# A two-block fp32 kernel on one core: last expert group summed in PSUM, GpSimd taken out of the combination, and another order in the MLP's last GEMM

## The chip, the cores and the metric

One core of a Trainium2 chip runs the whole program in one launch. The time is device microseconds (us) of one execution, the median of several; lower is better. The engines are PE (TensorE, matrix products), DVE (VectorE), ACT (ScalarE), POOL (GpSimd) and SP (SyncE, which here only issues transfers). All transfers of SP stand in one queue, those of POOL in another; an engine works through its own instructions in the order in which they were written for it.

## The reference, cut to what matters

The data are 512 rows of 1024 fp32 values. A first block mixes tokens and ends in a mixture of 64 experts (each row goes to 8 of them) beside a shared expert; a second block is attention and retention, and then an MLP with a squared ReLU.

```python
acc, _ = lax.scan(expert_block, jnp.zeros((N + 1, D), h.dtype), ...)   # rows gathered, SwiGLU, weighted, added back
f_lat = acc[:N] + swiglu(h, w_sh_gu, w_sh_down)
x_lat = x_lat + gt2 * rms_norm(f_lat, g_post_ffn)                      # end of block 1
...
h = x_lat
h = h + mixer_block(rmsnorm(h, norm_mix_gain), w_in, ...)              # block 2
h = h + jnp.square(jax.nn.relu(rmsnorm(h, norm_mlp_gain) @ w_ff1)) @ w_ff2
out = rmsnorm(h, norm_final_gain)
```

## The kernel before

**Products.** Every large product is made of three matmuls: each factor is split into a high part (`whi` for weights, written by ACT at L133; L153 for activations) and a low part (`wlo`, DVE L134; L154), and `mm3` adds high*high, low*high and high*low (L147 to L149). Weights come in units of 1 MB into a few buffers named `raw` (SP, L119), and a buffer is free for the next load when its unit is split. A unit splits in two pieces, so two `whi` and two `wlo` of 128x1024. The four tiles of 128 rows are numbered t = 0 to 3.

**End of the experts.** The experts run in groups. The outputs of a group (`ey`, 1024 columns a row) must be added to the rows that they came from. Columns 0 to 383 (`CA`) are added on PE: `expert_parts` splits them into `eys` (ACT and POOL), and a one-hot matrix `eoh` brings them into the PSUM tiles `acc[t]`. Columns 384 to 1023 go by indirect transfers of POOL that add into two tables `cb` in memory (L1076). Behind the last group stands a conditional loop for rows that found no place (`tc.If(total > 0)`, L1356 to L1359 in the profile), and then PE adds the shared expert's output product into `acc[t]` and a second PSUM tile `rest[t]` (48 matmuls of 128x512).

**The combination** is the start of the second block: for each tile the sums are put together from `acc[t]`, `rest[t]` (here `more[t]`) and the two reads of `cb` (into `cf` and `cg`), then normalised, scaled and added to the residual row `cx` (`x1[t]`), normalised again (`xn`), transposed on PE (`tp`, L1398) and split into the tiles `x`. It is written under `manual_schedule`: what each of DVE, ACT and POOL does there has the order of the code. `take(t)` empties PSUM, `norm(t)` scales and adds the residual, `normed_tile` makes `xn`, `turn_tile` transposes, `product(t, half)` is the first product of the block, with `w_v`. `rstd` is an inverse square root in 8 small DVE instructions for one column (11 for more).

```python
(nc.gpsimd if t else nc.vector).tensor_add(fs[t][:, CA:], fs[t][:, CA:], f2[t])
units = self.each_unit(wctx, self.quarters("w_v_2"), self.first_raws, [None, None, None, nc.gpsimd])
```

POOL so makes three of the four sums of the two tables (L1481), 384 of the 1024 columns of each residual add (`add2`, L1404) and the low part of the fourth `w_v` unit.

**The MLP** runs in four quarters of the hidden width. In each, `down` multiplies the hidden activations by a 1 MB x 4 block of `w_ff2` with seven products of half size (named 11, 3, 1, 2, 4, 12, 22) in place of eight. Sums of weight blocks are made by transfers that add into a loaded buffer (`plus`, issued by POOL, L1667). Products 11 and 2 collect in PSUM over the four quarters (`held`), the others are added to the output rows `h` quarter by quarter (`add`, L1682). In the last quarter the output is also squared (`ready`, `osq`, L1693), multiplied by the final gain (`gfin`, L1694), and each tile is scaled by its `rstd` (L1699 on DVE, L1700 on ACT) and sent out (SP, L1703, 8 transfers of 256 KB).

Of the kernel before, what the change touches and what calls it, by code (L numbers as in the profile page):

```python
# [11 lines left out]
F = mybir.dt.float32  # L12
R = mybir.dt.float32r
# [3 lines left out]
AF = mybir.ActivationFunctionType  # L17
OP = mybir.AluOpType
# [48 lines left out]
class Kernel:  # L67
# [1011 lines left out]

    def expert_parts(self, mp, y, row):  # L1080

        nc = self.nc
        m = row.shape[0]
        yh, yl = (mp.tile([128, CA], R, tag=f"eys{i}", name="eys", bufs=2)[0:m] for i in range(2))
        nc.scalar.activation(yh, y[0:m, :CA], AF.Copy)  # L1085
        last = nc.gpsimd.tensor_sub(yl, y[0:m, :CA], yh.bitcast(F))  # L1086
# [10 lines left out]
    def shared_expert(self, mp, pp, gp, gT, h2T):  # L1097
# [4 lines left out]
        for h in range(2):  # L1102
            hs = slice(h * H, (h + 1) * H)
            sg = []
            for u in range(2):
                for j in range(2):
# [9 lines left out]
                    yield  # L1116
    def shared_out(self, ps, gT, w, t, half):

        c = slice(half * 512, (half + 1) * 512)
        for i in range(2):  # L1120
            self.mm3(ps, [z[:, i, t * 128:(t + 1) * 128] for z in gT], [z[:, i, c] for z in w],
                     half == 1 and i == 0, i == 1)

# [86 lines left out]
    def experts(self, mp, pp, h2d, cb, acc, shared, gT, sums, grow, ahead, extra):  # L1210
# [84 lines left out]
        for t in range(NT):  # L1295
            nc.tensor.matmul(acc[t], zr[:, 0:128], zr, start=True, stop=False)
        late, sums = None, []
        for g in range(len(groups) + 1):
# [17 lines left out]
            def finish():  # L1316

                if not outs:
                    return
                e, parts = outs.pop(0)  # L1320
                lg = late[0]
                self.expert_out(pp, dn(e), [p[1:] for p in parts])
                last = None
                if not outs:
                    add()
                    for b, i in enumerate(rows_of[lg]):
                        s, last = self.expert_parts(mp, y[b], tabs[i][0])
                        sums.append(s)
# [44 lines left out]
        for t in range(NT):  # L1373
            self.shared_out(acc[t], gT, w, t, 0)
            rest.append(pp.tile([128, 512], F, tag="mm", name="mm", bufs=4))
            self.shared_out(rest[t], gT, w, t, 1)
        return rest
# [15 lines left out]
    def turn_tile(self, pp, xn, hi, lo, t):  # L1393
        ts = slice(t * 128, (t + 1) * 128)
        for u in range(2):
# [3 lines left out]
            self.split_ps(hi[:, 4 * u:4 * u + 4, ts], lo[:, 4 * u:4 * u + 4, ts], ps)  # L1399

    def add2(self, dst, a, b):

        for sl, e in ((slice(0, ADD_COLS), self.nc.vector), (slice(ADD_COLS, D), self.nc.gpsimd)):
            e.tensor_add(dst[:, sl], a[:, sl], b[:, sl])  # L1404

# [35 lines left out]
    def second_block(self, x1d, cb, acc, more, release):  # L1441
# [10 lines left out]
        with right("comb") as wp, ExitStack() as wctx:  # L1452
            fs = [wp.tile([128, D], F, name=f"cf{t}") for t in range(NT)]
            f2 = [wp.tile([128, D - CA], F, name=f"cg{t}") for t in range(NT)]

# [5 lines left out]
            def sums(t):  # L1461
                nc.sync.dma_start(fs[t][:, CA:], cb[0][rows[t], :])
                nc.sync.dma_start(f2[t], cb[1][rows[t], :])
# [7 lines left out]
            for t in range(1, NT):  # L1471
                nc.sync.dma_start(x1[t], x1d[rows[t], :])
            units = self.each_unit(wctx, self.quarters("w_v_2"), self.first_raws, [None, None, None, nc.gpsimd])
            ET = mybir.EngineType
            with tc.manual_schedule(engines={ET.DVE, ET.Activation, ET.Pool}):
                w = [next(units), next(units)]

                def take(t):

                    nc.scalar.activation(fs[t][:, 0:CA], acc[t][:, 0:CA], AF.Copy)  # L1480
                    (nc.gpsimd if t else nc.vector).tensor_add(fs[t][:, CA:], fs[t][:, CA:], f2[t])  # L1481
                    nc.vector.tensor_add(fs[t][:, CA:512], fs[t][:, CA:512], acc[t][:, CA:])
# [6 lines left out]
                take(0)  # L1489
                squares(fs[0], ss[:, 0:1])  # L1490
                nc.vector.tensor_mul(y, fs[0], g3)
# [4 lines left out]
                take(1)  # L1496
                xn = wp.tile([128, D], F, tag="xn", name="xn", bufs=2)
                nc.vector.tensor_scalar(xn, y, self.rstd(wp, ss0, D), None, op0=OP.mult)
                for t in range(2, NT):
                    take(t)  # L1500
                for t in range(1, NT):
                    squares(fs[t], ss[:, t:t + 1])
                release()
                pp = ctx.enter_context(tc.tile_pool(name="b2ps", bufs=1, space=PSUM))
                rs = self.rstd(wp, ss[:, 1:], D)
                self.turn_tile(pp, xn, xs[0], xs[1], 0)
                nc.sync.dma_start(xd[rows[0], :], x1[0])

                def norm(t):
                    nc.vector.scalar_tensor_tensor(fs[t], fs[t], rs[:, t - 1:t], g3, op0=OP.mult, op1=OP.mult)  # L1510
                    self.add2(x1[t], x1[t], fs[t])
                    nc.sync.dma_start(xd[rows[t], :], x1[t])
# [4 lines left out]

                norm(1)
                w.append(next(units))
                xn = self.normed_tile(wp, x1[1], gain)  # L1520
                w.append(next(units))
                w = [w[:2], w[2:]]
# [129 lines left out]
    def down(self, pp, rp, left, q, acc, held, gf):  # L1652
# [24 lines left out]

        def add(r, c, op, xs):
# [5 lines left out]
        def ready(r, c, last):  # L1684

            if q < 3:
                return
            for t in (2 * r, 2 * r + 1):
                if t not in ss:
                    ss[t] = rp.tile([128, 2], F, name=f"fss{t}")  # L1690
                a = acc[:, t, c * 512:(c + 1) * 512]
                sq = rp.tile([128, T], F, tag="relu", name="osq", bufs=6)
                nc.scalar.activation(sq, a, AF.Square, accum_out=ss[t][:, c:c + 1])  # L1693
                nc.vector.tensor_mul(a, a, gf[:, c * 512:(c + 1) * 512])  # L1694
                if last:
                    s = ss[t]
                    nc.vector.tensor_add(s[:, 0:1], s[:, 0:1], s[:, 1:2])
                    rs = self.rstd(rp, s[:, 0:1], D)
                    nc.vector.tensor_scalar(acc[:, t, 0:512], acc[:, t, 0:512], rs, None, op0=OP.mult)  # L1699
                    nc.scalar.activation(acc[:, t, 512:], acc[:, t, 512:], AF.Copy, scale=rs)  # L1700
                    for half in range(2):
                        sl = slice(half * 512, (half + 1) * 512)
                        nc.sync.dma_start(self.out[t * 128:(t + 1) * 128, sl], acc[:, t, sl])  # L1703

        e, f = load(0, 0), load(0, 1)
        plus(f, 1, 1)
        w = split(e)
        plus(e, 0, 1)
        product("11", w, held[0])
        z = product("3", split(f))  # L1710
        add(1, 1, "-", z)
        add(1, 0, "+", z)
        w = split(e)
        plus(e, 1, 1)
        z = product("1", w)
        add(1, 1, "-", z)
        add(0, 1, "-", z)
        w = split(e)
        plus(e, 1, 0)
        product("2", w, held[1])  # L1720
        if q == 3:
            add(0, 0, "+", held[0])
            x = [rp.tile([128, T], F, tag="relu", name="x", bufs=6) for _ in range(2)]
            for z, a, b in zip(x, *held):
                nc.scalar.activation(z, a, AF.Copy)
                nc.vector.tensor_add(z, b, z)
            add(1, 1, "-", x)
            ready(1, 1, False)
            add(0, 1, "-", x)
            add(1, 0, "+", x)  # L1730
        add(0, 1, "-", product("4", split(load(1, 1))))
        ready(0, 1, False)
        add(0, 0, "+", product("12", split(load(1, 0))))
        ready(0, 0, True)
        add(1, 0, "+", product("22", split(e)))
        ready(1, 0, True)

# [206 lines left out]
RAW3 = 2  # L1944
ADD_COLS = 640

# [141 lines left out]
```

## Time and profile before

| | |
|---|---|
| median of 3 runs | 2087.61 us (2087.3, 2087.61, 2090.02) |
| profiled execution: its time / its span in the profile | 2089.45 / 2087.7 us |
| granted clock of PE, mean (1.00 is 2.4 GHz) | 0.982 |
| PE busy | 1969.7 us, 94% of the span |
| DVE / ACT / POOL busy | 73% / 55% / 25% |

PE sets the pace nearly everywhere. The 118 us in which it is idle lie at the start and in a few joints between stages; the two places that the change touches are such joints.

### The profile page before, as it was taken

How to read it: one execution, taken by the hardware profiler on the slowest of the kernel's cores; microseconds unless marked ns; L12 is line 12 of the kernel's file. 1: busy time of each engine (PE TensorE's matmuls, PEld its weight loads, DVE VectorE, ACT ScalarE, POOL GpSimd, SP SyncE). 2: the span in 40 equal slices, each digit the busy share in tenths (PEclk: the TensorE clock that was granted, in tenths of full speed). 3: DMA queues.
4: the chain of work that ended last, by engine and by line, in shares of the span. 5: the costliest groups of instructions: out<-in, count | busy, mean ns of one | idle time of the engine just before them, and what ended most of it. 6: DMA issues, size and time to landing. Idle time of an engine off the chain costs nothing. (4 is left out here: it accounts for less than half of the span.)

```text
span 2087.7 us, 27579 instructions
## 1 busy us (share of the span) xinstructions
PE 1969.7 (94%) x9935; PEld 1583.8 (76%) x9935; DVE 1524.8 (73%) x2689; ACT 1156.2 (55%) x1734; POOL 512.1 (25%) x291
## 2 busy tenths in 40 slices
PE   7999999999889999899999996999999999999997
PEld 4877888787877677667766775777788888888886
DVE  6667766657899899899999997456863345755657
ACT  6544433233368798788888885334232324554554
POOL 0322221101236465445634323111100000000000
PEclk9999999999899999999999998999999999999999
DMA  7201126543489999899998997411122234546553
GB/s 294 80 22 43 68 98 252 212 166 132 168 302 349 312 343 351 284 353 340 353 347 306 330 333 252 143 61 61 41 91 91 99 143 134 159 126 197 123 140 81
DMA packets 73167, 406.03 MB, mean 194 GB/s; under 512 B 11758, under 2 KB 12735, under 8 KB 31428
## 3 DMA queue, kind: packets, MB, share of 16 engines
q1 hardware_dynamic: 58084, 360.18, 46.7%
q0 software_dynamic: 14944, 44.06, 9.7%
q8 instruction: 79, 1.29, 0.2%
q14 instruction: 60, 0.49, 0.1%
HBM read 388.07 MB, written 24.86 MB: 198 GB/s over the span
## 5 line engine op out<-in xcount | busy, mean ns | idle before, releaser
L134 DVE TENSOR_TENSOR wlo<-raw,whi 128x1024 fp32r<-128x1024 f32 x610 | 745.7, 1249 | 176.2 <-ACT whi L133 171.5
L133 ACT ACTIVATE whi<-raw 128x1024 fp32r<-128x1024 f32 x616 | 631.0, 1055 | 291.6 <-PE mm L148 178.5
L1076 POOL DMA_INDIRECT cb<-ey,sgi x67 | 151.6, 2262 | 158.8 <-ACT ey L1072 139.7
L1086 POOL TENSOR_TENSOR eys<-ey,eys 128x384 fp32r<-128x384 f32 (+2 forms) x47 | 102.9, 2191 | 126.4 <-ACT eys L1085 126.2
L147 PE MATMUL mm<-hT,whi 128*128 128x512 f32 x320 | 127.1, 397 | 0.6 <-DVE yb L369 0.6
L148 PE MATMUL mm<-hT,whi 128*128 128x512 f32 x320 | 125.9, 394 | 0.0
L149 PE MATMUL mm<-hT,wlo 128*128 128x512 f32 x320 | 125.5, 392 | 0.0
L148 PE MATMUL mm<-x,whi 128*128 128x512 f32 x304 | 122.5, 403 | 0.0
L147 PE MATMUL mm<-x,whi 128*128 128x512 f32 x304 | 120.9, 398 | 0.0
L149 PE MATMUL mm<-x,wlo 128*128 128x512 f32 x304 | 120.9, 398 | 0.0
L1034 PE MATMUL mm<-wlo,xT 128*128 128x512 f32 (+1 forms) x280 | 114.4, 409 | 4.1 <-DVE wlo L134 3.9
L1034 PE MATMUL mm<-whi,xT 128*128 128x512 f32 (+1 forms) x280 | 113.1, 404 | 0.3 <-ACT ey L1072 0.3
L148 PE MATMUL mm<-wlo,eaT 128*128 128x512 f32 (+2 forms) x268 | 106.6, 399 | 1.1 <-DVE wlo L134 0.9
L147 PE MATMUL mm<-whi,xT 128*96 128x512 f32 (+1 forms) x256 | 105.5, 412 | 0.3 <-DVE esum L1047 0.3
L148 PE MATMUL mm<-wlo,xT 128*96 128x512 f32 (+1 forms) x256 | 102.7, 401 | 3.1 <-DVE wlo L134 3.1
L149 PE MATMUL mm<-whi,eaT 128*128 128x512 f32 (+2 forms) x268 | 105.1, 394 | 0.0
L147 PE MATMUL mm<-whi,eaT 128*128 128x512 f32 (+2 forms) x268 | 101.7, 396 | 3.3 <-ACT eaT L153 1.7
L982 POOL DMA_INDIRECT xg<-h2d,sgi x47 | 79.8, 1699 | 97.9 <-issue 28.9
L147 PE MATMUL mm<-y,whi 128*128 128x512 f32 (+2 forms) x272 | 103.2, 379 | 0.0
L149 PE MATMUL mm<-y,wlo 128*128 128x512 f32 (+2 forms) x272 | 103.1, 379 | 0.0
L148 PE MATMUL mm<-y,whi 128*128 128x512 f32 (+2 forms) x272 | 103.1, 379 | 0.0
L149 PE MATMUL mm<-whi,xT 128*96 128x512 f32 (+1 forms) x256 | 101.3, 396 | 0.0
(591 smaller groups left out, 4684.9 us busy)
## 6 DMA issues: line engine op xcount, KB each, us to landing
raw<-in_w_expert_gu SPq DMA_DIRECT2D x128, 1024.0 KB
raw<-in_w_expert_down SPq DMA_DIRECT2D x64, 1024.0 KB
raw<-in_w_in SPq DMA_DIRECT2D x41, 1024.0 KB
raw<-in_w_ff SPq DMA_DIRECT2D x32, 1024.0 KB
raw<-in_w_ada SPq DMA_DIRECT2D x24, 1024.0 KB
raw<-in_w_ff POOLq DMA_DIRECT2D x16, 1024.0 KB
raw<-in_w_out SPq DMA_DIRECT2D x8, 1024.0 KB
raw<-in_w_v SPq DMA_DIRECT2D x4, 1024.0 KB
```

Of the source, the lines that this page charges most:

```text
L133: nc.scalar.activation(hi, rv[:, k:k + n], AF.Copy)
L134: (engine or nc.vector).tensor_sub(lo, rv[:, k:k + n], hi.bitcast(F))
L147: mm(ps, ah, bh, start=start, stop=False)
L148: mm(ps, ah, bl, start=False, stop=False)
L149: mm(ps, al, bh, start=False, stop=stop)
L982: self.nc.gpsimd.indirect_dma_start(out=xg[0:gi.shape[0]], out_offset=None, in_=h2d, in_offset=bass.IndirectOffsetOnAxis(ap=gi, axis=0), b ...
L1034: nc.tensor.matmul(ps[0:xT[0].shape[2]], xT[0][:, kk], z[:, k], start=kk == i == 0, stop=kk == KD - 1 and i == 1)
L1076: self.nc.gpsimd.indirect_dma_start(out=cb, out_offset=bass.IndirectOffsetOnAxis(ap=gi, axis=0), in_=y[p0:p1, CA:], in_offset=None, bounds ...
L1086: last = nc.gpsimd.tensor_sub(yl, y[0:m, :CA], yh.bitcast(F))
```

## The change

Part 1: if the last expert group is a single set of rows (here it has 96), all its 1024 columns are summed on PE (`whole`): ACT and DVE split them into `eyw`, nothing of this group goes to `cb`, and 16 matmuls of 128x512 behind the conditional loop (`ends`) take the place of 8 of 128x384 ahead of it. Part 2: in the combination POOL has no work any more. ACT alone empties PSUM, DVE makes the sums of the tables and all 1024 columns of the residual, squares and `rstd` are made tile by tile inside `norm`, and the third and fourth `w_v` units are split on DVE. Part 3: `down` has another order: the sums of weight blocks are made in the second buffer (`f`) in place of the first, products run as 11, 3, 2, 1, 4, 12, 22, and in the last quarter DVE and ACT follow the written order; one `rstd` serves two tiles, and the output leaves in 4 transfers of 512 KB.

```diff
-    def shared_out(self, ps, gT, w, t, half):
+    def shared_out(self, ps, gT, w, t, half, start):
...
+                if whole(lg):
+                    return
...
+            for half, ps in enumerate((acc[t], rest[t])):
+                for n, (oh, ys) in enumerate(ends):
+                    for i, y in enumerate(ys):
+                        nc.tensor.matmul(ps, oh[:, t * 128:(t + 1) * 128], y[:, half * 512:(half + 1) * 512],
+                                         start=half == 1 and n == i == 0, stop=False)
+                self.shared_out(ps, gT, w, t, half, half == 1 and not ends)
...
-            units = self.each_unit(wctx, self.quarters("w_v_2"), self.first_raws, [None, None, None, nc.gpsimd])
+            units = self.each_unit(wctx, self.quarters("w_v_2"), self.first_raws)
...
-                    nc.scalar.activation(fs[t][:, 0:CA], acc[t][:, 0:CA], AF.Copy)
-                    (nc.gpsimd if t else nc.vector).tensor_add(fs[t][:, CA:], fs[t][:, CA:], f2[t])
-                    nc.vector.tensor_add(fs[t][:, CA:512], fs[t][:, CA:512], acc[t][:, CA:])
-                    nc.vector.tensor_add(fs[t][:, 512:], fs[t][:, 512:], more[t])
+                    nc.scalar.activation(fs[t][:, 0:512], acc[t], AF.Copy)
+                    nc.scalar.activation(fs[t][:, 512:], more[t], AF.Copy)
+
+                def add(t):
+
+                    nc.vector.tensor_add(f1[t], f1[t], f2[t])
+                    nc.vector.tensor_add(fs[t][:, CA:], fs[t][:, CA:], f1[t])
...
+                def norm(t, between=None):
+                    add(t)
+                    squares(fs[t], ss[:, t:t + 1])
+                    if between:
+                        between()
+                    rs = self.rstd(wp, ss[:, t:t + 1], D)
+                    nc.vector.scalar_tensor_tensor(fs[t], fs[t], rs, g3, op0=OP.mult, op1=OP.mult)
+                    nc.vector.tensor_add(x1[t], x1[t], fs[t])
...
+            e, f = load(0, 0), load(0, 1)
+            plus(f, 1, 1)
+            w1, w3 = split(e), split(f)
+            plus(e, 0, 1)
+            plus(f, 0, 0)
+            product("11", w1, held[0])
+            w2 = split(f)
+            plus(f, 1, 0)
+            z = product("3", w3)
+            w = split(e)
...
+            for i in range(2):
+                t = 2 * r + i
+                if i:
+                    nc.vector.tensor_scalar(acc[:, t], acc[:, t], rs[:, i:i + 1], None, op0=OP.mult)
+                else:
+                    nc.scalar.activation(acc[:, t], acc[:, t], AF.Copy, scale=rs[:, i:i + 1])
+                nc.sync.dma_start(self.out[t * 128:(t + 1) * 128, :], acc[:, t])
```

How the instructions stand on three queues, before and after:

SP, behind the expert loop, where the last `w_v` load, the reads of `cb` and the first load of the attention's weights (`in_w_in`) are issued; before:

```order
L119 DMA raw<-in_w_v 128x2048
L1462 DMA cf_13584<-cb_93 128x640
L1463 DMA cg_13588<-cb_94 128x640
L1466 DMA g_13592<-g3d 128x1024
L1467 DMA cx_13593<-x1d 128x1024
```

and now:

```order
L119 DMA raw<-in_w_v 128x2048
L119 DMA raw<-in_w_in 128x2048
L1471 DMA cg_13595<-cb_93 128x640
L1472 DMA cg_13599<-cb_94 128x640
L1475 DMA g_13603<-g3d 128x1024
L1476 DMA cx_13604<-x1d 128x1024
```

The load of `in_w_in`, which stood behind the store `xd<-cx` of tile 0, has moved ahead of all reads of `cb`.

DVE, from the normalised tile 1 (`xn`) to the split of its transposed form (`x`), before:

```order
L1390 SCALAR_TENSOR_TENSOR xn<-cx_13595,rsy,gmix 128x1024
L1510 SCALAR_TENSOR_TENSOR cf_13587<-cf_13587,rsy,g_13592 128x1024
L1404 TENSOR_TENSOR cx_13596<-cx_13596,cf_13587 128x640
L154 TENSOR_TENSOR x_13576<-tp,x_13575 128x4x128 x2
L178 TENSOR_SCALAR rsx<-nss 128x1
```

and now (the line of dots stands for the other seven instructions of an `rstd`):

```order
L1404 SCALAR_TENSOR_TENSOR xn<-cx_13605,rsy,gmix 128x1024
L1494 TENSOR_TENSOR cg_13597<-cg_13597,cg_13601 128x640
L1495 TENSOR_TENSOR cf_13593<-cf_13593,cg_13597 128x640
L178 TENSOR_SCALAR rsx<-css 128x1
...
L1524 SCALAR_TENSOR_TENSOR cf_13593<-cf_13593,rsy,g_13603 128x1024
L1525 TENSOR_TENSOR cx_13606<-cx_13606,cf_13593 128x1024
L154 TENSOR_TENSOR x_13583<-tp,x_13582 128x4x128 x2
```

Between `xn` and the split of tile 1 stand now the sums of tile 2 and an `rstd` that needs ACT's squares of that tile.

DVE, the last instructions of the last `down`, before (the line of dots stands for small instructions of two `rstd`):

```order
L1694 TENSOR_TENSOR h<-h,gfin 128x512
L179 TENSOR_SCALAR rsy<-rsx 128x1
L1697 TENSOR_TENSOR fss_19599<-fss_19599 128x1
L182 SCALAR_TENSOR_TENSOR rsz<-rsy,rsx 128x1
L186 SCALAR_TENSOR_TENSOR rsy<-rsz,rsy 128x1
L1682 TENSOR_TENSOR h<-h,mm 128x512
...
```

and now:

```order
L1720 TENSOR_SCALAR h<-h,rsy 128x1024
L1695 TENSOR_TENSOR h<-h,mm 128x512
L1710 TENSOR_TENSOR h<-h,gfin 128x512
L1695 TENSOR_TENSOR h<-h,mm 128x512
L1710 TENSOR_TENSOR h<-h,gfin 128x512
L1715 TENSOR_TENSOR fss_19675<-fss_19675 128x2
```

Where the sums of the last product stood among the small instructions of the `rstd` of single tiles, both now stand together ahead of one `rstd` for two tiles.

## Rows read from the trace of the kernel before

**Rows 1.** Waits of PE, 1270 to 1350 us: total, times, longest.
```profile
PE tp L1398 <- DMA xd<-cx: 12.8, 1, 12.8
PE tp L1398 <- DVE xn L1390: 2.8, 1, 2.8
```

**Rows 2.** Waits of PE, 1750 to 2087 us.
```profile
PE tp L1398 <- DVE xn L1390: 0.3, 1, 0.3
```

**Rows 3.** Busy time by stretch: PE, PEld, DVE, ACT, POOL, clock, DMA share, GB/s.
```profile
1270.00:1280.00 10.00, 9.01 (x39) 6.93 (x37) 3.23 (x6) 1.64 (x3) 0.00 (x0) 1.00 0.94 328
1280.00:1290.00 10.00, 0.00 (x0) 0.00 (x0) 9.41 (x21) 3.44 (x7) 5.41 (x3) 0.62 1.04 413
...
1350.00:1750.00 400.00, 395.24 (x1860) 317.71 (x1859) 218.69 (x427) 127.96 (x214) 36.08 (x26) 1.00 0.25 86
```

**Rows 4.** SP's issues, timeline: start, duration, instruction.
```profile
1256.71 10.99 SPq L119 DMA_DIRECT2D raw<-in_w_v  x4
1271.10 0.33 SPq L1462 DMA_DIRECT2D cf<-cb  x1
```

**Rows 5.** DVE's timeline, end of the experts to the transposed tile 1.
```profile
1268.92 1.22 DVE L134 TENSOR_TENSOR wlo<-raw,whi 128x1024 fp32r<-128x1024 f32 x1 [0.44 <-DVEq L1356]
1276.76 0.82 DVE L1481 TENSOR_TENSOR cf<-cf,cg 128x640 f32<-128x640 f32 x1 [6.62 <-DMA cg<-cb]
...
1279.85 0.15 DVE L178 TENSOR_SCALAR rsx<-css 128x1 f32<-128x1 f32 x1
...
1281.57 1.28 DVE L714 SCALAR_TENSOR_TENSOR cx<-rv,rsy,cx 128x1024 f32<-128x1024 f32 x1
1282.89 2.50 DVE L1495 TENSOR_TENSOR rv<-cx,gmix 128x1024 f32<-128x1024 f32 x1
...
1289.23 0.75 DVE L1498 TENSOR_SCALAR xn<-rv,rsy 128x1024 f32<-128x1024 f32 x1
...
1293.30 0.17 DVE L178 TENSOR_SCALAR rsx<-css 128x3 f32<-128x3 f32 x1 [1.73 <-ACT rv L1486]
...
1295.36 1.28 DVE L154 TENSOR_TENSOR x<-tp,x 128x512 fp32r<-128x512 f32 x2
...
1310.79 1.28 DVE L154 TENSOR_TENSOR x<-tp,x 128x512 fp32r<-128x512 f32 x2
```

**Rows 6.** POOL's timeline in the same stretch.
```profile
1282.77 5.50 POOL L1481 TENSOR_TENSOR cf<-cf,cg 128x640 f32<-128x640 f32 x3 [15.63 <-DMA cf<-cb]
```

**Rows 7.** ACT's timeline: one square of a tile.
```profile
1290.89 1.06 ACT L1486 ACTIVATE rv<-cf 128x1024 f32<-128x1024 f32 x1 [3.44 <-DVE cf L1483]
```

**Rows 8.** PE's timeline: three idle times and the matmuls behind them.
```profile
1278.62 0.39 PE L149 MATMUL mm<-whi,shT 128*128 128x512 f32 x1
1291.78 1.94 PE L1398 MATMUL tp<-ident,xn 128*128 128x128 f32 x8 [12.77 <-DMA xd<-cx]
...
1308.96 1.27 PE L1398 MATMUL tp<-ident,xn 128*128 128x128 f32 x8 [2.83 <-DVE xn L1390]
...
854.76 1.01 PE L1095 MATMUL acc<-eys,eoh 96*128 96x384 f32 x2 [6.39 <-POOL eys L1086]
855.57 0.63 PE L1034 MATMUL mm<-wlo,xT 128*128 128x512 f32 x1
...
859.41 0.40 PE L148 MATMUL mm<-wlo,xT 128*128 128x512 f32 x1
```

**Rows 9.** PE's timeline, the last matmul.
```profile
2074.06 0.39 PE L149 MATMUL mm<-whi,hdx2l 128*128 128x512 f32 x1
```

**Rows 10.** ACT's timeline in the last quarter.
```profile
2048.17 5.80 ACT L133 ACTIVATE whi<-raw 128x1024 fp32r<-128x1024 f32 x6 [5.00 <-DMA raw<-in_w_ff]
...
2077.57 0.63 ACT L1693 ACTIVATE osq<-h 128x512 f32<-128x512 f32 x1 [1.42 <-DVE h L1682]
...
2083.16 0.72 ACT L1700 ACTIVATE h<-h,rsy 128x512 f32<-128x512 f32 x1 [1.56 <-DVE rsy L186]
```

**Rows 11.** POOL's timeline, an adding transfer of the last quarter.
```profile
2040.26 0.86 POOL L1667 DMA_DIRECT2D raw<-in_w_ff  x1 [22.36 <-DVE hd1l L154]
```

More of the change, by code (lines that the diff above doesn't have):

```diff
@@ L1078, in expert_send, with expert_parts @@
                                           compute_op=OP.add)
-    def expert_parts(self, mp, y, row):
+    def expert_parts(self, mp, y, row, whole=False):
         nc = self.nc
         m = row.shape[0]
-        yh, yl = (mp.tile([128, CA], R, tag=f"eys{i}", name="eys", bufs=2)[0:m] for i in range(2))
-        nc.scalar.activation(yh, y[0:m, :CA], AF.Copy)
-        last = nc.gpsimd.tensor_sub(yl, y[0:m, :CA], yh.bitcast(F))
+        if whole:
+            yh, yl = (mp.tile([128, D], R, tag="ey", name="eyw", bufs=3)[0:m] for _ in range(2))
+            for c in range(0, D, 512):
+                sl = slice(c, c + 512)
+                nc.scalar.activation(yh[:, sl], y[0:m, sl], AF.Copy)
+                last = nc.vector.tensor_sub(yl[:, sl], y[0:m, sl], yh[:, sl].bitcast(F))
+        else:
+            yh, yl = (mp.tile([128, CA], R, tag=f"eys{i}", name="eys", bufs=2)[0:m] for i in range(2))
+            nc.scalar.activation(yh, y[0:m, :CA], AF.Copy)
+            last = nc.gpsimd.tensor_sub(yl, y[0:m, :CA], yh.bitcast(F))
         oh = mp.tile([128, T], R, tag="eoh", name="eoh", bufs=2)[0:m]
@@ L1116, in shared_expert @@
                     yield
-    def shared_out(self, ps, gT, w, t, half):
+    def shared_out(self, ps, gT, w, t, half, start):
         c = slice(half * 512, (half + 1) * 512)
         for i in range(2):
-            self.mm3(ps, [z[:, i, t * 128:(t + 1) * 128] for z in gT], [z[:, i, c] for z in w],
-                     half == 1 and i == 0, i == 1)
+            self.mm3(ps, [z[:, i, t * 128:(t + 1) * 128] for z in gT], [z[:, i, c] for z in w], start and i == 0, i == 1)
     def first_block(self):
@@ L1296, in experts @@
             nc.tensor.matmul(acc[t], zr[:, 0:128], zr, start=True, stop=False)
-        late, sums = None, []
+        late, sums, ends = None, [], []
+        whole = lambda g: g == len(groups) - 1 and len(groups[g][1]) == 1
         for g in range(len(groups) + 1):
@@ L1326, in finish @@
                     for b, i in enumerate(rows_of[lg]):
-                        s, last = self.expert_parts(mp, y[b], tabs[i][0])
-                        sums.append(s)
+                        s, last = self.expert_parts(mp, y[b], tabs[i][0], whole(lg))
+                        (ends if whole(lg) else sums).append(s)
+                if whole(lg):
+                    return
                 with tc.issue_after(last.ins) if last else ExitStack():
@@ L1453, in second_block @@
             fs = [wp.tile([128, D], F, name=f"cf{t}") for t in range(NT)]
-            f2 = [wp.tile([128, D - CA], F, name=f"cg{t}") for t in range(NT)]
+            f1, f2 = ([wp.tile([128, D - CA], F, name=f"cg{i}{t}") for t in range(NT)] for i in range(2))
             sq, y = vr[:, 3], vr[:, 2]
@@ L1489, in second_block @@
                 take(0)
+                add(0)
                 squares(fs[0], ss[:, 0:1])
+                for t in range(1, NT):
+                    take(t)
+                release()
+                pp = ctx.enter_context(tc.tile_pool(name="b2ps", bufs=1, space=PSUM))
                 nc.vector.tensor_mul(y, fs[0], g3)
@@ L1676, in product, with add @@
             return pss
-        def add(r, c, op, xs):
+        def add(r, c, op, xs, then=None):
             for i, x in enumerate(xs):
@@ L1682, in add @@
                 (nc.vector.tensor_add if op == "+" else nc.vector.tensor_sub)(a, a, x)
[L1684 to L1736, printed above, removed]
+                if then:
+                    then(2 * r + i)
+        def ready(c):
+            return lambda t: squares(t, c)
+        def squares(t, c):
+            r, i = divmod(t, 2)
+            if r not in ss:
+                ss[r] = rp.tile([128, 2, 2], F, name=f"fss{r}")
+            a = acc[:, t, c * 512:(c + 1) * 512]
+            sq = rp.tile([128, T], F, tag="relu", name="osq", bufs=6)
+            nc.scalar.activation(sq, a, AF.Square, accum_out=ss[r][:, c, i:i + 1])
+            nc.vector.tensor_mul(a, a, gf[:, c * 512:(c + 1) * 512])
@@ new lines, in down @@
+        ET = mybir.EngineType
+        end = q == 3
+        with self.tc.manual_schedule(engines={ET.DVE, ET.Activation}) if end else ExitStack():
+            e, f = load(0, 0), load(0, 1)
[8 more added lines that the diff above has]
+            w = split(e)
+            add(1, 1, "-", z)
+            add(1, 0, "+", z)
+            product("2", w2, held[1])
+            w4 = split(load(1, 1))
+            if end:
+                add(0, 0, "+", held[0])
+                x = [rp.tile([128, T], F, tag="relu", name="x", bufs=6) for _ in range(2)]
+                for z, a in zip(x, held[0]):
+                    nc.scalar.activation(z, a, AF.Copy)
+            z1 = product("1", w)
+            z4 = product("4", w4)
+            wg = split(load(1, 0))
+            if end:
+                for z, b in zip(x, held[1]):
+                    nc.vector.tensor_add(z, b, z)
+                add(0, 1, "-", x)
+                add(1, 1, "-", x)
+            add(0, 1, "-", z1)
+            add(1, 1, "-", z1, end and ready(1))
+            if end:
+                add(1, 0, "+", x)
+            wl = split(f)
+            add(0, 1, "-", z4, end and ready(1))
+            add(0, 0, "+", product("12", wg), end and ready(0))
+            if end:
+                result(0)
+            add(1, 0, "+", product("22", wl), end and ready(0))
+            if end:
+                result(1)
@@ L1944 @@
 RAW3 = 2
-ADD_COLS = 640
 CA = 384
```

26 lines of the change are left out of this document (7 added, 19 removed).

## The prediction

> **What bounds the kernel now.** I read the page first (PE busy 94% of the span), then PE's waits by stretch, since only a place where PE waits, or the end behind its last matmul, can give or cost time. Between 1270 and 1350 us PE waits twice, 12.8 us for the first transposition of the combination and 2.8 us for the second [rows 1]; from 1750 us to the end it waits 0.3 us in all [rows 2]. So there are two places to cost. The combination is a chain of DVE and ACT from the landing of the `cb` tables to `xn` (the wait view names the store of `cx` as releaser of the first transposition, but the last reader of the PSUM that the transposition needs is `take(3)` on DVE, which ends just ahead of it). The tail lies behind the last matmul, which ends at 2074.06 + 0.39 = 2074.45 [rows 9] in a span of 2087.7: 13.25 us of DVE, ACT and the output. In the MLP between them PE is never late, so no order of `down` can gain there; it can only lose.
>
> **The change, part 1: where the tables land.** Before, SP issues the first read of `cb` at 1271.10 [rows 4] and DVE has both tables at 1276.76, 5.66 us later [rows 5]. Now a load of 1 MB stands ahead of the reads, and it needs the buffer of a `w_v` unit to be split. DVE's last split piece behind the conditional loop ends at 1268.92 + 1.22 = 1270.14 [rows 5]; the two `eyw` pieces push one more `wlo` behind the loop, so the unit is split 1.2 us later, 1271.3, and the reads are issued at about 1271.7, 0.6 us later than before. What the 1 MB ahead costs no row shows. Below, nothing: the transfers of this queue already overlap, and the last group's own adding transfer is gone; the tables land at 1276.76. Above, the whole MB passes first at the 328 GB/s of this stretch [rows 3], 3.2 us, so 1276.76 + 0.6 + 3.2 = 1280.5. I take the middle, X = 1278.6, since the queue was also full before (a `w_v` load was 4 us old when the reads were issued).
>
> The Trainium skill, "DMA: Bandwidth & Descriptors", section "Queues, rings and completion order", says that on each transfer engine the descriptors of one issuing queue are consumed in ring order. Taken strictly, that gives the upper bound. The trace of before has no large load directly ahead of a waited-for read, so it can't decide here; it is the third rival below.
>
> **Part 2: from X to the first transposition.** DVE and ACT must do: two sums of 640 columns (0.82 each, 1.64), a square (1.06 [rows 7] and its read-out, 1.25), `rstd` (from 1279.85 to 1281.57 [rows 5], 1.72), the residual (1.28), the next square (1.25), `rstd` (1.72) and `xn` (0.75 [rows 5]): 9.6, with half a microsecond of hand-overs 10.1. The multiply by the gain lies beside the square: it took 2.50 us while POOL made its three sums of 5.50 us [rows 5, 6], where a `wlo` of the same 1024 columns takes 1.22, so POOL's work had cost it 1.3 us; that is gone. PSUM is emptied by ACT early: the shared products, now 64 matmuls in place of 48, end 16 x 0.23 = 3.7 us after the last one of before (1278.62 [rows 8]), less about 0.7 because 8 matmuls ahead of the loop are gone: 1282, and `take(3)` ends by 1283. So the first transposition comes at 1278.6 + 10.1 = 1288.7, in place of 1291.78: 3.1 us gained. An earlier X gives little more: behind `take(3)` ACT's square, `rstd` and `xn` still take 3.7, so it can't start before 1286.7.
>
> **Part 3: from the first to the second transposition, and what gives it back.** DVE now has more to do between them: the split of tile 0 (3.0 with the transposition), sums of tile 1 (1.6), ACT's square and the first `whi` (2.3, since the third `w_v` unit waits for ACT behind that square), two `wlo` (2.4), `rstd` (1.7), scale and residual (2.5), two `wlo` of the unit that POOL had (2.4), `rstd` (1.7), `xn` (1.3): 18.9 us, against 1308.96 - 1291.78 = 17.2 before [rows 8]. The second transposition so comes at 1307.6, 1.4 us earlier than before. But then the split of the transposed tile 1, which stood 3.3 us behind the start of `xn` (1310.79 [rows 5]), has to let pass on DVE: the sums of tile 2 (1.6), ACT's square (1.25), `rstd` (1.7), scale and residual (2.5), 7 us. It ends its first half at 1315.2. Before, the nine last products of tile 0 stood behind the second transposition and kept PE at work (at half clock) until about 1313.3, when tile 1 was there; now all 48 stand ahead of it, PE has nothing else, and tile 1's products start at 1315.3, 2.0 us later. PE has then been idle, but for eight transpositions, since 1306, and restarts at the low clock: after an idle time of 6.39 us at 854.76 the matmuls took 0.63 in place of 0.40 (1.2 in place of 2.4 GHz) until 859.41 [rows 8], 4.65 us of half speed, 2.3 us lost. About 1.0 comes back, since two products that need only the high part of tile 1 run early and one matmul fewer stands before the third transposition. Sum of the combination: 2.0 + 2.3 - 1.0 = **+3.3 us**; with the bounds of X (-1.8, +1.9) +1.5 to +5.2. In the attention behind it PE is busy 395.24 of 400 us [rows 3], so the shift stays.
>
> **Part 4: the tail.** The last product ends as before, 2074.45. DVE is free of the older work then (two `rstd` chains and four scalings less), so both last sums stand at 2073.85 and 2075.1 (the second waits for its PSUM and the first `gfin`), the last `gfin` ends at 2076.3, ACT's square (0.63 [rows 10] and 0.18) at 2076.55. One `rstd` of eleven small instructions takes 2.1 (from 1293.30 to 1295.36 [rows 5]) and a sum of 0.2 stands ahead: 2078.9. Then ACT scales 1024 columns, estimated at 1.15 from 0.72 for 512 [rows 10], DVE 0.75: ready at 2080.1. Before, ACT was ready at 2083.16 + 0.72 = 2083.88 [rows 10], and the span ended 3.8 us later. Now the last two tiles (1 MB) leave together where 0.5 MB did: 0.5 MB more at 413 GB/s [rows 3] is 1.3, at 328 GB/s 1.6. End: 2080.1 + 3.8 + 1.4 = 2085.3, **-2.4 us**; bounds -1.0 (DVE a microsecond late, slower output) to -3.0.
>
> **Part 5: the four `down` before that end** I cost at nothing. An adding transfer lands 7.9 us after its issue (2040.26 to ACT's release at 2048.17 [rows 10, 11]). The sum for product 2 is issued behind the split of unit 3, near 2027.6, and lands near 2035.5; its split is done by 2038, product 2 starts near 2047. The cover is thus 9 us in the last quarter. The loads and adding transfers per quarter are as many as before.
>
> Sum: 3.3 - 2.4 = +0.9 on a span of 2087.7. The profiled execution took 2089.45, 1.84 over the median; the shift is taken on the median: 2087.61 + 0.9 = **2088.5 us**. Its own range, by the bounds above: 2086.1 to 2091.8.
>
> **Rivals.**
> 1. *Faster, 0.15: tile 1 does not wait so long.* If X is at its lower bound (+1.5) and the idle time ahead of tile 1's products, broken by the transpositions, does not cost the clock (-2.3), and the tail gives 3.0, the sum is -3.8: 2083.8. For it: half of that idle time lies on either side of the transpositions. Against: before, an idle time of only 2.83 us ahead of 1308.96 [rows 1, 8] was followed by slow matmuls.
> 2. *Slower, 0.16: a split in `down` waits for an adding transfer.* Place: ACT, `whi` of product 2; behind it on ACT stand the activations of the hidden products. In each quarter three accumulations into `f` now follow each other, each 7.9 us and each behind a split. In quarters 0 to 2 ACT and DVE have no written order, and I have shown the cover only for the last. If PE waits 1.5 us in each of four quarters, +6: 2094.5. It decides once such a transfer lands later than some 3 us ahead of its product.
> 3. *No change, 0.15: the 1 MB passes whole ahead of the tables*, X = 1280.5, +5.2 - 2.4 = +2.8: 2090.4; with the tail's smallest gain it becomes +4.2 and slower.
> 4. *No change, 0.12: the tail's gain is eaten by the larger last transfers* or by the sums waiting: +3.3 - 0.5: 2090.4.
>
> The Trainium skill, "SBUF — State Buffer", section "Who interferes with whom", says that a DVE instruction with two SBUF inputs contends with a GpSimd instruction that reads SBUF. By it all that POOL gave up would be gain on DVE; the row of 2.50 us agrees, and part 2 shows how little of it is left behind `take(3)` and the tables.
>
> **How the numbers follow.** What this measurement can tell from no change is 0.2%, 4.2 us. The forecast has 0.42, spread within 2086.1 to 2091.8, all of it "same". Faster by over 0.2% (below 2083.4) takes most of rival 1 alone: 0.14. Slower (above 2091.8) takes rival 2, a third of rivals 3 and 4: 0.25. Same 0.61. The range goes from rival 1's 2083.8 to 2094.0, just short of rival 2's full price.
>
> **What the profile after would show.** Right: the first `cg` sum of DVE at 1278 to 1279, the first transposition near 1288.7, a PE wait of some 7 us ahead of tile 1's products with a low clock behind it, the first matmuls of the attention 3 us later; no wait of PE in the MLP; last scalings near 2080 and four output transfers. Wrong: PE waits after 1750 us, the first sum after 1280.5 or before 1276.8, or a low clock missing behind that wait.

## The result and the profile after

The changed kernel takes 2103.26 us (median of 5 runs, 2100.04 to 2108.15), the kernel before 2087.42 in the same count of runs: ratio 1.0076, interval 1.0058 to 1.0094, about 16 us slower. The prediction was 2088.5 us (2083.8 to 2094.0); the time lies above its range. The profiled execution took 2103.26 us with a span of 2101.5.

The first view is PE's waits in the combination (total, times, longest), to be held against [rows 1]:

```profile
PE tp L1412 <- issue: 14.4, 1, 14.4
PE mm L149 <- DVE x L154: 3.1, 1, 3.1
PE mm L148 <- DVE wlo L134: 2.4, 1, 2.4
PE mm L147 <- ACT x L153: 1.8, 1, 1.8
PE acc L1102 <- ACT eys L1092: 1.5, 1, 1.5
PE mm L1388 <- DVEq L1366: 1.1, 1, 1.1
```

The wait ahead of the first transposition is longer, 14.4 against 12.8, though PE works 3.2 us longer behind the loop ahead of it (to 1280.76, 13.3 us behind DVE's first `wlo` there, against 10.1 before [rows 5, 8]). The waits 3.1 and 1.8 are those of tile 1 that the prediction had; the wait of 2.4 is for the low part of a weight unit that POOL had split before, when PE had no such wait [rows 1]. "issue" names no releaser, so what is late has to be looked for upstream: in SP's queue.

SP's waits, and SP's issues in the same stretch (start, duration), to be held against [rows 4]:

```profile
SPq L1526 <- DVE cx L1525: 13.4, 2, 9.6
SPq L1471 <- PE mm L1388: 8.7, 1, 8.7
SPq L119 <- DVEq L1366: 3.3, 1, 3.3
```

```profile
1254.98 12.63 SPq L119 DMA_DIRECT2D raw<-in_w_v  x4
1269.86 0.33 SPq L119 DMA_DIRECT2D raw<-in_w_in  x1
1279.50 0.33 SPq L1471 DMA_DIRECT2D cg<-cb  x1
```

Here is the loss: the first read of `cb` (L1471) stands in SP's queue for 8.7 us until a matmul of L1388, one of the 16 that sum the last group from `eyw` and its one-hot matrix. It was expected near 1271.7 and goes out at 1279.50. PE's rows show which matmul released it, and what comes behind:

```profile
1278.74 0.63 PE L1388 MATMUL mm<-eyw,eoh 96*128 96x512 f32 x2
...
1280.37 0.39 PE L149 MATMUL mm<-whi,shT 128*128 128x512 f32 x1
1295.20 1.94 PE L1412 MATMUL tp<-ident,xn 128*128 128x128 f32 x8 [14.44 <-issue]
...
1314.17 1.40 PE L1412 MATMUL tp<-ident,xn 128*128 128x128 f32 x8 [0.27 <-DVE xn L1404]
...
1321.82 0.80 PE L149 MATMUL mm<-whi,x 128*128 128x512 f32 x1 [3.08 <-DVE x L154]
```

It is the last pair, which ends near 1279.4. DVE gets the tables, and ACT empties the first tile of PSUM (the memory in which PE's sums collect) into `cf`, only behind it:

```profile
1267.47 2.36 DVE L134 TENSOR_TENSOR wlo<-raw,whi 128x1024 fp32r<-128x1024 f32 x2 [0.21 <-DVEq L1366]
1283.54 0.83 DVE L1494 TENSOR_TENSOR cg<-cg,cg 128x640 f32<-128x640 f32 x1 [13.71 <-DMA cg<-cb]
...
1287.10 1.23 DVE L1508 TENSOR_TENSOR rv<-cf,g 128x1024 f32<-128x1024 f32 x1 [1.80 <-DMA g<-g3d]
```

```profile
1279.52 0.60 ACT L1489 ACTIVATE cf<-acc 128x512 f32<-128x512 f32 x1 [12.60 <-PE mm L1388]
```

ACT could have read `acc[0]` more than ten microseconds earlier, since its sums were complete by 1266.4; it is the tile `cf` that it writes which could not be used yet, as with SP and `cg`. Both tiles come from a pool (a stretch of memory that is taken and given back as a whole). The trace shows nine semaphore instructions at the line of the reads, of which the longest took 8728 ns:

```profile
L1471 SPq EVENT_SEMAPHORE  x9: 28/28/8728, 1270.2 to 1279.4; - x9
```

In the program built from this kernel they stand ahead of the first read and name the engines and queues that used the memory earlier, PE among them. There the tile of that read and `cf` share no byte with `eyw` or its one-hot matrix; only their pools overlap (`comb` of the combination, `moe` of the experts). So the wait is for the last user of the earlier pool and not for these tiles' own bytes; this is read from the built program, and no run separates the two.

I measure the combination from DVE's first `wlo` behind the loop to the first matmul of the attention, since profiled executions differ by some us in what lies ahead: 1267.47 to 1357.40, 89.9 us, against 1268.92 [rows 5] to 1347.97, 79.05. That is 10.9 us. PE's timelines, after and then before:

```profile
1357.40 0.39 PE L147 MATMUL mm<-x,whi 128*128 128x512 f32 x1
```

```profile
1347.97 0.39 PE L147 MATMUL mm<-x,whi 128*128 128x512 f32 x1
```

The other part is at the end. PE's last matmul ends at 2083.68 + 0.39 = 2084.07, so 17.4 us lie behind it in place of 13.25 [rows 9]. DVE's timeline there:

```profile
2081.68 0.68 DVE L1695 TENSOR_TENSOR h<-h,mm 128x512 f32<-128x512 f32 x1
2083.22 0.69 DVE L1710 TENSOR_TENSOR h<-h,gfin 128x512 f32<-128x512 f32 x1 [0.85 <-ACT osq L1709]
2083.83 0.68 DVE L1695 TENSOR_TENSOR h<-h,mm 128x512 f32<-128x512 f32 x1
2085.35 0.69 DVE L1710 TENSOR_TENSOR h<-h,gfin 128x512 f32<-128x512 f32 x1 [0.85 <-ACT osq L1709]
...
2090.46 0.69 DVE L1710 TENSOR_TENSOR h<-h,gfin 128x512 f32<-128x512 f32 x1 [0.79 <-ACT osq L1709]
2091.07 0.68 DVE L1695 TENSOR_TENSOR h<-h,mm 128x512 f32<-128x512 f32 x1
2092.53 0.69 DVE L1710 TENSOR_TENSOR h<-h,gfin 128x512 f32<-128x512 f32 x1 [0.79 <-ACT osq L1709]
...
2095.49 0.75 DVE L1720 TENSOR_SCALAR h<-h,rsy 128x1024 f32<-128x1024 f32 x1
```

Each multiply by `gfin` waits 0.8 us for ACT's square: it overwrites the values that the square reads. In the written order nothing stands between sum, square and multiply, so each of eight tile halves takes 2.1 us of DVE. In the kernel before, the order left free put other instructions between them, and the longest such wait from 2064 us on was 0.25:

```profile
2071.88 0.69 DVE L1694 TENSOR_TENSOR h<-h,gfin 128x512 f32<-128x512 f32 x1 [0.25 <-ACT osq L1693]
```

Between the first matmul of the attention and the end of the last one lie 726.67 us, against 726.48 before, with one wait of PE of 0.8 us (its PSUM tile not yet added by the late DVE): nothing is lost in the MLP itself.

### The profile page after: what moved, and what is told of

Its sections match the earlier page's. It is cut to its first block, busy times and chain, and to the rows that moved or that the text cites. A ratio compares the mean times of both kernels' runs of the same rounds, so it can differ in the third digit from the quotient of the medians.

```text
span 2101.5 us, 27561 instructions
## 1 busy us (share of the span) xinstructions
PE 1974.1 (94%) x9943; PEld 1586.2 (75%) x9943; DVE 1525.3 (73%) x2691; ACT 1159.9 (55%) x1737; POOL 491.5 (23%) x281
```

## The experiments

Gains and losses are told as ratios to the kernel before, 0.1% being 2.1 us. Each ratio is taken against runs of the kernel before that were made beside it, and can lie some 2 us from what the two medians give. "Tail" is the span less the end of the last matmul; "combination" is the stretch defined above.

**e1, the combination alone**: the changed kernel with `down` of before.

> The changed end of the experts and combination (parts 1 and 2) with the down of before. Theory 1 (two separate losses, read from the trace after: about 11 us in the combination, because the reads of cb wait on SP for the last matmul that reads eyw, and about 4.4 us in the tail, because the in-place gfin multiply waits for ACT's square): 2087.4 + 11 = 2098.5 us, with the end behind the last matmul 13.3 us long as before, and the reads of cb again near 8 us late. Rival (one loss that the two parts make only together, or that lies in the earlier quarters): within 4 us of 2087.

Ratio 1.0053 (1.0033 to 1.0072): 11 us. The medians differ by 8.8 us (2098.45 against 2089.67). The combination takes 89.06 us, 10.0 more than before, the tail 13.1, and the wait is there again:

```profile
SPq L1471 <- PE mm L1388: 8.7, 1, 8.7
```

**e2, `down` alone** on the kernel before.

> The kernel before with only down in its new order. Theory 1: slower by the tail alone, 2087.4 + 4.4 = 2091.8 us, with some 17.4 us behind the last matmul in place of 13.3 and DVE waiting about 0.8 us for ACT's osq ahead of each of eight gfin multiplies. Rival (the adding transfers make PE wait in the quarters): PE waits of over 1 us between 1750 us and the last matmul, and the end behind it unchanged.

Ratio 1.0022 (1.0011 to 1.0033), 4.6 us. The tail takes 17.35 us. PE waits from 1750 us on are 0.8 and 0.3 us, so the adding transfers hold nothing up. The two losses, 11 and 4.6, add up to the 15.8 of both, within intervals of about 4 and 2 us to either side.

**e3, the last group's matmuls first.**

```diff
-        for t in range(NT):
...
-            for half, ps in enumerate((acc[t], rest[t])):
...
+        for half, pss in enumerate((acc, rest)):
+            for t in range(NT):
                 for n, (oh, ys) in enumerate(ends):
                     for i, y in enumerate(ys):
...
+                        nc.tensor.matmul(pss[t], oh[:, t * 128:(t + 1) * 128], y[:, half * 512:(half + 1) * 512],
                                          start=half == 1 and n == i == 0, stop=False)
+        for t in range(NT):
+            for half, ps in enumerate((acc[t], rest[t])):
                 self.shared_out(ps, gT, w, t, half, half == 1 and not ends)
```

> The changed kernel with all 16 matmuls of the last group ahead of the 48 shared ones, in place of two ahead of each six. Theory 1 (SP holds the reads of cb until the last matmul that reads eyw or its one-hot matrix, since the tiles of the combination lie in their memory): that matmul now ends near 1269.5 in place of 1279.4, the reads are issued near 1270.5, DVE has the first tables at 1275 to 1277 in place of 1283.5, and the time falls by 6.5 to 8 us, to about 2096. Rival (the 1 MB of in_w_in ahead of the reads in the queue is what delays them): the reads land no earlier than 1280, gain at most 3.5 us.

Ratio 1.0042 (1.0027 to 1.0057), 7 us less than the changed kernel, and its combination takes 82.9 us in place of 89.9. Its timeline runs some 3.5 us later from the start. SP's waits and issue, DVE's first `wlo` and first table sum, PE's transpositions and tile 1:

```profile
SPq L1472 <- DMA raw<-in_w_in: 1.2, 1, 1.2
...
SPq L1472 <- PE mm L1387: 0.6, 1, 0.6
```

```profile
1274.89 0.33 SPq L1472 DMA_DIRECT2D cg<-cb  x1
```

```profile
1271.02 2.36 DVE L134 TENSOR_TENSOR wlo<-raw,whi 128x1024 fp32r<-128x1024 f32 x2 [0.21 <-DVEq L1366]
1281.35 0.82 DVE L1495 TENSOR_TENSOR cg<-cg,cg 128x640 f32<-128x640 f32 x1 [7.97 <-DMA cg<-cb]
```

```profile
1291.56 1.94 PE L1413 MATMUL tp<-ident,xn 128*128 128x128 f32 x8 [4.38 <-issue]
...
1310.56 1.07 PE L1413 MATMUL tp<-ident,xn 128*128 128x128 f32 x8 [1.34 <-DVE xn L1405]
...
1318.21 0.79 PE L149 MATMUL mm<-whi,x 128*128 128x512 f32 x1 [3.23 <-DVE x L154]
```

The wait for the group's matmuls has shrunk to 0.6 us; the tables are there 10.3 us behind the first `wlo`, in place of 16.1. Moving the last reader and nothing else brought the reads forward, so it was that reader that they waited for. ACT's first copy into `cf` now waits for the sums in `acc[0]`, its own data, and no more for L1387. The expected landing at 1275 to 1277 (on the scale of the changed kernel) was too early: it is 1277.8, 6.5 us behind the issue, with the 1 MB ahead of it; in the changed kernel, where that load had long landed, 4.0 us.

**e4, the multiplies behind both squares.**

```diff
-                if then:
-                    then(2 * r + i)
+            if then:
+                for i in range(2):
+                    then(2 * r + i)
+                for i in range(2):
+                    a = acc[:, 2 * r + i, c * 512:(c + 1) * 512]
+                    nc.vector.tensor_mul(a, a, gf[:, c * 512:(c + 1) * 512])
...
-            nc.vector.tensor_mul(a, a, gf[:, c * 512:(c + 1) * 512])
```

> The changed kernel, but in the last quarter the two sums of a product come first, then the two squares, then the two gfin multiplies. Theory 1 (the in-place multiply waits for ACT's square of the same values, 0.8 us of DVE idle eight times): the second sum covers most of the first square, so about 1.2 us less for each of four pairs; the end behind the last matmul falls from 17.4 to about 12.5 us and the time by 4 to 5 us, to about 2098.5. Rival (larger output transfers or the one rstd for two tiles make the tail long): gain under 1.5 us.

Ratio 1.0053 (1.0035 to 1.0072), 4.8 us less than the changed kernel; the two intervals overlap, but the tail of the profile says the same: 12.6 us in place of 17.4. DVE's last pairs:

```profile
2081.70 1.30 DVE L1701 TENSOR_TENSOR h<-h,gfin 128x512 f32<-128x512 f32 x2 [0.26 <-ACT osq L1713]
...
2085.28 0.75 DVE L1723 TENSOR_SCALAR h<-h,rsy 128x1024 f32<-128x1024 f32 x1
2085.95 1.28 DVE L1695 TENSOR_TENSOR h<-h,mm 128x512 f32<-128x512 f32 x2
2087.42 1.30 DVE L1701 TENSOR_TENSOR h<-h,gfin 128x512 f32<-128x512 f32 x2 [0.19 <-ACT osq L1713]
```

A wait of 0.2 for a pair stands where two of 0.8 stood.

**e5, e3 and e4 together.**

> The changed kernel with the edits of e3 and e4 together (all matmuls of the last group ahead of the shared ones; the gfin multiplies behind the two squares). Theory 1 (two separate losses): the gains add, about 7.0 + 4.8 us, ratio to the kernel before about 1.002 (1.000 to 1.004). What would be left is what the prediction had: about +3.3 us from tile 1's wait in the combination, and a tail now 0.7 us shorter than before. Rival (one loss hides the other): ratio above 1.004.

Ratio 1.0015 (1.0005 to 1.0024), as expected: the two losses are independent as far as the intervals tell, and what is left is about 3 us. Its combination takes 82.4 us, 3.3 more than before.

**e6, tile 1's split earlier.** In `norm(1)` the sums of tile 2 follow those of tile 1 at once, and in the loop only the `rstd` of the next tile stands ahead of the split; ACT's squares move with the sums. The lines of the loop:

```diff
-                        norm(t + 2)
+                        rs = root(t + 2)
...
                     product(t, 1, turn)
                     if t + 2 < NT:
+                        norm(t + 2, rs)
+                        if t + 3 < NT:
+                            add(t + 3)
                         xn = self.normed_tile(wp, x1[t + 2], gain)
+                        if t + 3 < NT:
+                            squares(fs[t + 3], ss[:, t + 3:t + 4])
```

> e5 with another order in the combination: the table sums of the tile after next are made while DVE waits for ACT, and the split of the transposed tile stands ahead of the scaling and residual of the tile after it. Theory 1 (PE waits for the low part of tile 1, 26.6 us behind the first transposition, and restarts at the low clock): tile 1's products start 4 to 5 us earlier behind the second transposition and the time falls by 4 to 6 us against e5, to a ratio of 0.999 to 1.000. Rival (the next tile's xn comes later by as much and PE waits there instead): gain under 1.5 us, with a wait of over 2 us ahead of the third transposition.

Ratio 0.9981 (0.9970 to 0.9991), faster than the kernel before and 7 us less than e5; the medians give 6.0 (2085.30 against 2091.32) and the combination, 76.3 us, gives 6.1, the upper end of what was expected. PE doesn't wait for the split of tile 1 any more, nor ahead of the third transposition. It still waits 3.3 us for the low part that POOL had made before.

**e7, the reads of `cb` ahead of the 1 MB load** (on e5), and **e8, e6 and e7 together.** SP's loads of the attention are ordered behind the second tile's read.

```diff
+            with tc.issue_after(read.ins):
+                self.attention(xs, w_in, pp, atT)
```

> e5 with the 1 MB load of in_w_in issued behind the reads of cb for tiles 0 and 1, as before, in place of ahead of them. Rival 3 of the prediction (the 1 MB passes ahead of the tables): the first tables land 2 to 2.5 us earlier against the loop's end, and if the chain from them is what sets the first transposition, the time falls by 2 to 2.5 us. Theory 1b (take(3) and the square of tile 0 on ACT behind it set the first transposition): the tables land earlier, but the time moves by less than 0.7 us.

> e6 with the reads ahead of the load as in e7. If the gains of e6 and e7 add: e6's ratio less 0 to 0.001; a candidate for a version faster than the kernel before (0.998 to 1.000).

In the profile of e7 the tables come 7.75 us behind the first `wlo`, 2.6 earlier than in e5 (10.3), and the combination takes 79.9 us, 2.5 less. The time doesn't show it: 1.0017 (1.0008 to 1.0025) against 1.0015. e8 has 0.9980 (0.9970 to 0.9990) against 0.9981 of e6, its combination 75.45 against 76.3. So the load ahead does delay the tables by 2.6 us: 1.1 is a later issue of the first read (3.33 us behind the first `wlo` in e5, 2.20 in e7), and 1.5 a longer way from that issue to DVE's sum (7.0 against 5.55), where the prediction gave 0 to 3.2. But what the kernel gains from its removal is not settled: the intervals are as wide as the gain.

**e9, part 1 undone** on e8 (`whole` never true).

> e8, but the last expert group goes the way of the others again (384 columns by PE ahead of the loop, the rest to cb): part 1 undone, the rest of e8 kept. If part 1 is worth nothing by itself: the shared products end some 3.7 us earlier, the reads of cb wait for the group's adding transfer as before (landing near 1276.8 on the scale of the kernel before), and the time lies within 2 us of e8. If summing the group in PSUM is what makes e8 fast: slower than e8 by 2 to 4 us.

Ratio 0.9971 (0.9960 to 0.9982), 2082.51 us, the fastest of all, though its interval overlaps e8's. The combination takes 73.3 us. So the last group in PSUM shows no gain: without it the reads wait for the group's adding transfer, on SP's waits

```profile
SPq L1472 <- DMA cb<-ey,sgi: 3.6, 1, 3.6
```

and the shared products are done 10.1 us behind DVE's first `wlo`, in place of 13.3 in the changed kernel. Tile 1's products now follow the second transposition at once:

```profile
1304.16 1.03 PE L1413 MATMUL tp<-ident,xn 128*128 128x128 f32 x8
1305.45 0.50 PE L147 MATMUL mm<-whi,x 128*128 128x512 f32 x1 [0.25 <-ACT x L153]
```

**e11 and e12, a second profile of e7's and of e9's kernel**, for the clock (see the last section).

> The kernel of e7 once more, for a second profiled execution. In the profiles of e3, e6 and e8 the clock falls to its lower level for some 6 us behind the short waits of PE at the loop's end (0.84 to 0.96 and 1.13 to 1.16 us), in those of e5, e7 and the changed kernel it does not. Theory (it is a matter of the execution, not of the kernel, and it hides e7's gain in part of the timed runs): this profile may show the fall; if so the shared products end about 16 us behind DVE's first wlo in place of 13.3 and the first transposition comes at about 20.5 in place of 17.7. If the clock stays up, 17.7 again, and nothing is learnt on it.

> The kernel of e9 once more. PE waits at the loop's end for 0.17 and 0.92 us only, so the clock should stay up, the first transposition come 18 to 18.5 us behind DVE's first wlo, and the combination take 73 to 74 us as in e9. If the clock falls here too, the fall does not hang on the waits that part 1 brings.

In neither did the clock fall. e11 has the first transposition 18.0 us behind DVE's first `wlo` and a combination of 81.4 us (e7: 17.7 and 79.9), which makes e7's gain over e5 smaller, 1.0 us; it took 2090.33 us, one execution. e12 has 74.1 us (e9: 73.3) and took 2080.03; its first transposition comes 19.2 us behind the first `wlo`, where 18 to 18.5 was expected. Whether a falling clock hides e7's gain in the timed runs so stays open.

**e10, the mended `down` alone** on the kernel before.

> The kernel before with only the new down, and the gfin multiplies behind the two squares as in e4. Theory 1 (the order of products and adding transfers costs nothing, the waits for ACT's squares were all of e2's loss): ratio 0.999 to 1.000, the end behind the last matmul 12.5 us against 13.3. Rival (something else in down costs as well): ratio above 1.0015.

Ratio 0.9996 (0.9987 to 1.0005): no measurable difference, tail 12.4 us. The new order of products, adding transfers and outputs costs and gains nothing.

## Why the prediction was wrong

**Part 1, where the tables land: the step that failed.** It said that the reads are issued "at about 1271.7", taking the `in_w_in` load ahead of them as the only new thing on SP. They were issued at 1279.50, because they wait for the last reader of `eyw`. The pool of the combination takes over memory of the pool that the expert stage's tiles were in, and the change gave that pool a later last use: before, PE had read `eys` to the end by 1266.3 (PE's timeline of before); now it reads `eyw` and the one-hot matrix until 1279.4. The prediction asked of each moved transfer what stands ahead of it in its queue, but not what the pool that it writes into still waits for. That the load of `in_w_in` had moved ahead of the reads in SP's order was probably a trace of just this wait; that is only argued. e3 took 7 of the 11 us away by the place of 16 matmuls, and with the wait gone the step's own sum was nearly right: the tables of e3 land 10.33 us behind DVE's first `wlo` of the loop's end, which on the scale of the kernel before [rows 5] is 1268.92 + 10.33 = 1279.25, against X = 1278.6. Two of the prediction's own signs of being wrong came: the first sum stood at 1283.54, after 1280.5, and PE waited 0.8 us in the MLP, for a reason that belongs to part 4.

**Parts 2 and 3 held in their sums, with one wait misplaced.** From the first table sum to the first transposition 10.1 was forecast; e3 shows 1291.56 - 1281.35 = 10.2 (in the changed kernel 11.7, because the gain `g`, queued behind the reads, came late as well). To the second transposition 18.9: 18.97 in the changed kernel, 19.0 in e3. To tile 1's products 26.6: 26.62 and 26.65. But the wait of "some 7 us" was not one of tile 1 alone: 2.4 us of it stood in the middle of tile 0's products, for the fourth unit's low part, and only 0.3, 1.8 and 3.1 at tile 1. The prediction had that low part on DVE's list and not among PE's waits, so that the sum came out so close is in part luck. The clock fell behind both, as it said for one (matmuls of 0.63 us from 1311.57 and from 1322.41). The loss of the combination without the wait, +3.3: e3 shows 82.86 - 79.05 = 3.8, e5 3.3. e6 shows that tile 1's wait makes up this loss: with the split earlier it became a gain of 2.8 us against before. What POOL's work had cost DVE is gone: the multiply by the gain took 1.22 us in the changed kernel, where it had taken 2.50 [rows 5]. The rule of the Trainium skill that the prediction weighed ("SBUF — State Buffer", "Who interferes with whom") agrees with both rows. As the prediction said, not all of it reached the first transposition: in e3 that comes 2.3 us earlier behind the first `wlo` than before (20.5 against 22.9), since the tables come 2.5 later.

**Part 4, the tail: the second step that failed, of sign.** It let the last `gfin` end at 2076.3, ahead of the end of ACT's square of the same values (2076.55). In place, the multiply has to wait for the square. Instead of -2.4 the tail cost 17.4 - 13.25 = +4.2. The mended order (e4, e5, e10) gives 12.4 to 12.6, a gain of 0.7 to 0.8: still a third of the forecast, in the main because in e4 DVE reaches the sums of the last product at 2085.95, 1.5 us behind its end, held by the scaling of the first two tiles.

**Part 5 held**, and with it rival 2 fell: no wait in the quarters but 0.8 us, caused by the tail's own DVE. Rival 3 had the right place and the wrong cause: the load ahead costs 2.6 us of landing (e5 against e7), 1.5 of it behind the issue; the wait cost more than three times the 2.6. By the Trainium skill ("DMA: Bandwidth & Descriptors", "Queues, rings and completion order") the descriptors of one queue are consumed in ring order on each transfer engine, from which the prediction had its upper bound of 3.2; the 1.5 lie below it, but the load had been issued 0.9 us ahead of the read, so the runs don't decide on that rule. None of the rivals had the wait for the pool or for ACT's square.

## What to carry to other kernels

When a change lets an engine read a buffer later, ask which pool takes over the memory of that buffer's pool: here the first transfer and the first copy into tiles of the next stage waited for the last reader, though by the built program their own bytes lay elsewhere, and the reads behind that transfer in SP's queue waited with it. Put such last reads ahead of other work of the same engine (16 matmuls moved, 7 us). When an order is fixed by hand, look for in-place updates: between the sum, its reader on another engine and the update stand other instructions, or the engine idles for the reader's whole duration each time.

## What was not expected of the hardware

The clock at the loop's end differs from one execution to the next. In e3, e6 and e8, PE ran at the lower clock (matmuls of 0.63 in place of 0.39 us, 1.2 in place of 2.4 GHz) for about 6 us (e3, e8) and 3.5 us (e6) behind two waits of 0.8 to 1.2 us; in e5, whose program differs from e3's there in nothing, and in e7, e11 and the changed kernel, it did not. PE's rows of e3 and then of e5:

```profile
1267.98 1.89 PE L1387 MATMUL acc<-eyw,eoh 96*128 96x512 f32 x7 [0.96 <-DVE eyw L1089]
1271.00 3.75 PE L1387 MATMUL mm<-eyw,eoh 96*128 96x512 f32 x8 [1.13 <-DVEq L1366]
1274.55 0.63 PE L147 MATMUL acc<-whi,shT 128*128 128x512 f32 x1
...
1277.45 0.39 PE L148 MATMUL mm<-wlo,shT 128*128 128x512 f32 x1
```

```profile
1265.24 1.89 PE L1387 MATMUL acc<-eyw,eoh 96*128 96x512 f32 x7 [1.00 <-DVE eyw L1089]
1268.26 2.06 PE L1387 MATMUL mm<-eyw,eoh 96*128 96x512 f32 x8 [1.13 <-DVEq L1366]
```

Waits of nearly the same length, 3.75 us for eight matmuls in the one and 2.06 in the other. The shared products then end 16.2 us behind DVE's first `wlo` in e3 and 13.3 in e5, though the first transposition comes at nearly the same place, 20.5 and 20.3. It may be part of why the changed kernel's runs spread over 8 us; that was not tested. Besides, a read of the tables took 4.0 us from its issue to DVE's sum with no load under way (1279.50 to 1283.54) and 6.5 with a 1 MB load issued 1.5 us ahead of it (e3, 1274.89 to 1281.35); in e7, with that load behind the reads but the last `w_v` loads ahead of them, 5.55.
